# A pair of experts in the two column halves of TensorE, on whole float32 weights

## The chip, the cores and the metric

The kernel runs on one core of one Trainium2 chip. The metric is the device time of one execution in microseconds; a number of executions are timed, and one more is profiled. Products run on TensorE (PE, its weight loads PEld), the rest on VectorE (DVE), ScalarE (ACT) and GpSimd (POOL); SyncE (SP) issues the transfers.

## What is computed

Two transformer-like blocks on 512 tokens of 1024 features. The change lies in the last layer of the second block, an expert layer in which each of 16 experts takes the 64 tokens that have the greatest affinity to it. Cut to that layer:

```python
def expert_choice_ffn(h, w_router, w_gate, w_up, w_down):
    cap = EC_CAPACITY * L // N_EXPERTS                 # 2 * 512 // 16 = 64
    aff = jax.nn.softmax((h @ w_router).astype(jnp.float32), axis=-1)
    top_aff, top_idx = lax.top_k(jnp.swapaxes(aff, 1, 2), cap)
    xe = jax.vmap(lambda hb, ib: hb[ib])(h, top_idx)
    hid = jax.nn.silu(jnp.einsum('becd,edf->becf', xe, w_gate)) * jnp.einsum('becd,edf->becf', xe, w_up)
    ye = jnp.einsum('becf,efd->becd', hid, w_down) * top_aff[..., None].astype(h.dtype)
    combine = lambda ib, yb: jnp.zeros((L, D), yb.dtype).at[ib.reshape(-1)].add(yb.reshape(-1, D))
    return jax.vmap(combine)(top_idx, ye)
```

Each expert has three float32 matrices of 1024 x 1024 (gate, up, down), 201.3 MB for all 16.

## The kernel before

The residual stream lies with features on the partitions, in eight tiles `g.x` of 128 x 512. `moe` (line 1380) gets it tile by tile from `mixer_out` (line 1326), the output projection of the mixer ahead, and squares and scales each tile as it comes. Then the router's logits, the norm, and `route` (line 1343): softmax, the 64 greatest tokens of each expert by eight rounds of MAX8 and MATCH_REPLACE8, and by a scan the place of each token in each expert's list. The normed tokens are turned so that tokens lie on the partitions, in an upper part `e_ht` and a lower part `xh` (line 1473).

All large products of the kernel run in the one-pass format (float32r): an operand is split into an upper part, exact in that format, and a lower part, the rest (`split`, line 36: a copy on ScalarE, a subtraction on VectorE). The experts do it so:

- `stream` (line 1417) issues the weights in pieces of 256 rows (1 MiB, two row tiles `k`) into five places, two of the pool `wraw` and three of `e_raw`, and splits each row tile of 128 x 1024 into `whi` and `wlo`; `prepare` keeps three row tiles ahead of their use. The last two row tiles of each down matrix stay whole. A row tile is called a chunk below.
- `gather` (line 1482) makes one-hot tiles `e_oh` for the two experts of a pair and picks their tokens by products with `e_ht` and `xh`; the upper and the lower part of an expert's 64 tokens lie side by side as 128 stationary columns, in `e_x`. `turn` (line 1505) turns the one-hot tiles for later use and sorts the affinities.
- `product` (line 1521) makes [128, 1024] in two PSUM banks from eight row tiles: for a split tile 4 products of 128 stationary and 512 moving columns (upper and lower part of the weights, two halves `h` of the output), for a whole tile 2 products of 64 stationary columns, in float32. The two parts of an expert's rows come out on partitions 0 to 63 and 64 to 127.
- `activate` (line 1543) adds these two parts and turns them with products against a matrix `pair` (line 1549), makes silu(gate) * up with features on the partitions (silu by tanh) and splits the result into `e_hid`.
- The down product of an expert is scaled by the affinity on eviction and split into `xl` (lines 1589, 1590); `combine` (line 1561) adds a pair's rows to their tokens, per feature tile 4 products with the turned one-hot tiles `e_oht` and one accumulation on VectorE (line 1568).

The loop (line 1575) goes expert by expert: gate and up of expert e, then down of expert e - 1. `gather`, `turn`, `activate` and `combine` are generators in the queue `side`; `product` calls `side.pump()` after every second row tile, so that they come between the large products. A scheduler then sets the final order on each engine. `final` (line 1596) is the last norm and the stores.

## Time and profile before

| | us |
|---|---|
| median of 3 runs | 3245.01 |
| lowest, highest | 3242.98, 3249.72 |
| span of the profiled execution | 3242.7 |

| engine | busy us | share of the span |
|---|---|---|
| PE | 3108.6 | 96% |
| PEld | 2567.7 | 79% |
| DVE | 2098.0 | 65% |
| ACT | 1301.8 | 40% |
| POOL | 330.6 | 10% |

The span runs from the first to the last instruction of the profiled execution. That execution's own device time is not listed apart from its span; the three timed runs lie 0.3 to 7.0 us above the span, their median 2.3 us. "Busy" is the union of an engine's instructions; matmuls are pipelined and their ends are modelled, so a busy PE need not be at its peak, and the distance between starts tells its pace. DMA share is the mean busy share of the 16 DMA engines. The experts' stage is the last sixth of the span; the first five sixths are the first block and the mixer of the second.

### The profile page before, as it was taken

The numbers are of one execution on the slowest core, as the hardware profiler recorded it, in microseconds if no ns is written. First come the engines' busy times: TensorE is split into PE (matmuls) and PEld (weight loads), VectorE is DVE, ScalarE is ACT, GpSimd is POOL, SyncE is SP. The second block draws the span as 40 slices with busy tenths as digits, with TensorE's granted clock in tenths as the row PEclk, the third lists the DMA queues.
The fourth block names the chain that finished last, engine by engine and source line by source line (L and its number), as shares of the span: only waits on it lengthen the run. The fifth ranks groups of instructions, "written<-read, shape, count | busy, mean of one in ns | idle before, by whom it ended". The sixth has DMA issues, their size and how long they took to land. (4 is left out here: it accounts for less than half of the span.)

```text
span 3242.7 us, 40377 instructions
## 1 busy us (share of the span) xinstructions
PE 3108.6 (96%) x15866; PEld 2567.7 (79%) x15866; DVE 2098.0 (65%) x3258; ACT 1301.8 (40%) x1928; POOL 330.6 (10%) x256
## 2 busy tenths in 40 slices
PE   7999999999999999999998999999999789999997
PEld 6888888778888888887876888887889677777775
DVE  4444557654455896456766664447656569888887
ACT  3222335332223322233534322224322367777775
POOL 0101121010110020113102012011000210000000
PEclk9999999999999999999999999999999779999998
DMA  4432432123322674244212332223323249999995
GB/s 141 127 104 91 137 118 88 56 65 100 95 92 91 208 246 156 91 137 131 66 65 89 105 110 76 83 82 113 95 84 95 91 158 362 336 338 343 343 347 211
DMA packets 315347, 475.68 MB, mean 147 GB/s; under 512 B 32223, under 2 KB 244959, under 8 KB 312084
## 3 DMA queue, kind: packets, MB, share of 16 engines
q1 hardware_dynamic: 311768, 467.32, 42.8%
q10 hardware_dynamic: 2748, 3.68, 0.4%
q8 instruction: 124, 2.03, 0.3%
q0 software_dynamic: 640, 2.10, 0.2%
q14 instruction: 67, 0.55, 0.1%
HBM read 453.38 MB, written 19.67 MB: 146 GB/s over the span
## 5 line engine op out<-in xcount | busy, mean ns | idle before, releaser
L38 ACT CAST whi<-wraw 128x1024 fp32r<-128x1024 f32 (+4 forms) x532 | 535.0, 1016 | 1158.6 <-PE mm L68 892.3
L67 PE MATMUL mm<-xh,whi 128*128 128x512 f32 x1952 | 774.6, 399 | 11.2 <-ACT xh L135 8.3
L68 PE MATMUL mm<-xl,whi 128*128 128x512 f32 x1952 | 771.3, 395 | 0.8 <-DVE xl L136 0.6
L69 PE MATMUL mm<-xh,wlo 128*128 128x512 f32 x1952 | 768.7, 394 | 1.1 <-DVE wlo L39 1.1
L39 DVE TENSOR_TENSOR wlo<-wraw,whi 128x1024 fp32r<-128x1024 f32 (+4 forms) x532 | 680.9, 1289 | 110.1 <-ACT whi L38 93.9
L67 PEld LDWEIGHTS mm<-xh,whi 128*128 128x128 f32 x1952 | 371.1, 191 | 99.9 <-ACT xh L135 9.2
L68 PEld LDWEIGHTS mm<-xl,whi 128*128 128x128 f32 x1952 | 370.9, 190 | 80.4 <-issue 2.5
L69 PEld LDWEIGHTS mm<-xh,wlo 128*128 128x128 f32 x1952 | 371.0, 190 | 77.9 <-DVE wlo L39 1.9
L67 PE MATMUL mm<-hh,whi 128*128 128x512 f32 x704 | 278.8, 396 | 0.0
L69 PE MATMUL mm<-hh,wlo 128*128 128x512 f32 x704 | 277.9, 395 | 0.0
L68 PE MATMUL mm<-hl,whi 128*128 128x512 f32 x704 | 276.1, 392 | 0.0
L39 DVE TENSOR_TENSOR wlo<-e_raw,whi 128x1024 fp32r<-128x1024 f32 x210 | 249.2, 1221 | 32.5 <-ACT whi L38 31.8
L38 ACT CAST whi<-e_raw 128x1024 fp32r<-128x1024 f32 x210 | 212.3, 1050 | 31.1 <-PE mm L1531 29.0
L181 POOL TENSOR_TENSOR x<-x,dt 128x512 f32<-128x512 f32 x72 | 117.3, 1629 | 945.1 <-DVE dt L180 925.4
L161 DVE TENSOR_TENSOR gs<-mm,rb 128x512 f32<-128x512 f32 x88 | 60.8, 690 | 211.0 <-PE mm L69 206.6
L166 DVE TENSOR_TENSOR gs<-gs,mm 128x512 f32<-128x512 f32 x88 | 60.4, 686 | 194.0 <-PE mm L69 193.9
L180 DVE SCALAR_TENSOR_TENSOR dt<-mm,rb 128x512 f32<-128x512 f32 x104 | 71.8, 690 | 174.3 <-PE mm L69 174.2
L1531 PE MATMUL mm<-wlo,e_x 128*128 128x512 f32 x512 | 167.3, 408 | 2.1 <-DVE wlo L39 2.1
L1531 PE MATMUL mm<-whi,e_x 128*128 128x512 f32 x512 | 166.5, 407 | 1.6 <-DVE e_x L1501 1.3
L69 PEld LDWEIGHTS mm<-hh,wlo 128*128 128x128 f32 x704 | 132.2, 188 | 30.7
L68 PEld LDWEIGHTS mm<-hl,whi 128*128 128x128 f32 x704 | 132.3, 188 | 30.3 <-DVE hl L39 0.3
L67 PEld LDWEIGHTS mm<-hh,whi 128*128 128x128 f32 x704 | 132.4, 188 | 28.3
(623 smaller groups left out, 4630.4 us busy)
## 6 DMA issues: line engine op xcount, KB each, us to landing
wraw<-ffn_gate SPq DMA_DIRECT2D x44, 1024.0 KB, 5.4
wraw<-ffn_up SPq DMA_DIRECT2D x44, 1024.0 KB, 5.4
wraw<-w_in SPq DMA_DIRECT2D x38, 1024.0 KB, 5.3
e_raw<-e_gate SPq DMA_DIRECT2D x38, 1024.0 KB, 6.3
e_raw<-e_up SPq DMA_DIRECT2D x38, 1024.0 KB, 7.0
e_raw<-e_down SPq DMA_DIRECT2D x38, 1024.0 KB, 7.1
wraw<-e_gate SPq DMA_DIRECT2D x26, 1024.0 KB, 6.3
wraw<-e_up SPq DMA_DIRECT2D x26, 1024.0 KB, 6.9
```

The lines of the kernel that those rows point to most:

```text
L38: g.nc.scalar.copy(hi, src)
L39: g.nc.vector.tensor_sub(lo, src, f32(hi))
L67: g.nc.tensor.matmul(out, lh, rh, start=(i == 0), stop=False)
L68: g.nc.tensor.matmul(out, lh, rl, start=False, stop=False)
L69: g.nc.tensor.matmul(out, ll, rh, start=False, stop=(i == n - 1))
L161: nc.vector.tensor_mul(gs, pg, rb)
L166: nc.vector.tensor_mul(gs, gs, pu)
L180: nc.vector.scalar_tensor_tensor(t, pd, 0.25, rb, op0=OP.mult, op1=OP.mult)
L181: (nc.vector if c0 + nch == sum(groups) else nc.gpsimd).tensor_add(g.x[2 * c + m], g.x[2 * c + m], t)
L1531: nc.tensor.matmul(o, l, part[:, h * 512:(h + 1) * 512], start=(k + i == 0), stop=(k == NK - 1 and i == len(parts) - 1), skip_group_check= ...
```

## The change

Two experts, 2b and 2b + 1, form a pair b and work at the same time, expert 2b with 64 stationary columns in the left half of the array (output on partitions 0 to 63), expert 2b + 1 in the right half (partitions 64 to 127). Their weights are used whole, in float32, without a split. The inputs are laid out so that row tile k of both experts is one contiguous piece of 1 MiB, 8 KB on each partition (`host_inputs`). `load` has 12 places for such chunks: seven of `e_raw`, two of `wraw`, and three pairs of `whi` and `wlo` (two transfers each); the first loads are issued while `mixer_out` still runs. The tokens `ht` are float32 in one part, and the gather of a pair makes 128 columns, 64 of each expert. silu(gate) * up is made on token rows straight from the PSUM banks and turned by transposes (`turn_hidden`). A pair needs one turn of its one-hot tiles and, per feature tile, 2 products in `combine`. The gather and the turn of the first pair stand wholly ahead of the first product. `side.pump()` is called after every chunk.

```diff
+NR = 7
 def moe(g, I, P, x_out):
...
+    def load():
+        n = len(loaded)
+        w, b, k = chunks[n]
+        src = I["e_" + w][b, k]
+        place = n % (NR + 5) - (NR - 2)
+        if place < 2 or place >= 5:
+            raw = g.wraw.tile([128, 8 * WC], F32, name="wraw")[:, :2 * D] if 0 <= place < 2 else place_of()
+            raw = raw.rearrange("p (j c) -> p j c", j=2)
+            nc.sync.dma_start(raw, src)
+            loaded.append([raw[:, 0], raw[:, 1]])
+        else:
+            raw = [g.wsp.tile([128, 4 * WC], F32, name=nm)[:, :D] for nm in ("whi", "wlo")]
+            for j in range(2):
+                nc.sync.dma_start(raw[j], src[:, j])
+            loaded.append(raw)
...
+        if k in (1, 3, 5):
+            while len(loaded) < (NR - 2) * (k + 1) // 6:
+                load()
...
-        if k < 2:
-            nc.scalar.activation(xh[:, k, :], xw[k], AF.Identity, bias=shift[:, k:k + 1])
-            nc.vector.scalar_tensor_tensor(xl[:, k, :], xw[k], shift[:, k:k + 1], f32(xh[:, k, :]), op0=OP.add,
-                                           op1=OP.subtract)
-        else:
-            nc.scalar.activation(xw[k], xw[k], AF.Identity, bias=shift[:, k:k + 1])
-            nc.scalar.copy(xh[:, k, :], xw[k])
-            nc.gpsimd.tensor_sub(xl[:, k, :], xw[k], f32(xh[:, k, :]))
+        nc.scalar.activation(xw[k], xw[k], AF.Identity, bias=shift[:, k:k + 1])
...
     def gather(b):
...
+            for k in range(4):
+                f = 4 * q + k
+                for i in range(NT):
+                    nc.tensor.matmul(p[:, k * 128:(k + 1) * 128], ht[:, i, f * 128:(f + 1) * 128],
+                                     oh[:, i].rearrange("p j c -> p (j c)"), start=(i == 0), stop=(i == NT - 1))
...
+    def product(lhs):
         ps = [g.ps_m.tile([128, 512], F32, name="mm") for _ in range(2)]
         for k in range(NK):
-            prepare()
-            parts = ahead.pop(0)
-            for i, part in enumerate(parts):
-                for h in range(2):
-                    o, l = (ps[h], lhs(k)) if len(parts) > 1 else (ps[h][0:64], full(k))
-                    nc.tensor.matmul(o, l, part[:, h * 512:(h + 1) * 512], start=(k + i == 0),
-                                     stop=(k == NK - 1 and i == len(parts) - 1), skip_group_check=True)
-            if k % 2:
-                side.pump()
+            if used[0] == len(loaded):
+                load()
+            raw = loaded[used[0]]
+            used[0] += 1
+            for h in range(2):
+                for j in range(2):
+                    nc.tensor.matmul(ps[h][pj[j], :], lhs(k, j), raw[j][:, h * 512:(h + 1) * 512], start=(k == 0),
+                                     stop=(k == NK - 1), skip_group_check=True)
+            side.pump()
         return ps
...
+            pg = product(lambda k, j: xe[b][:, k, j, :])
+            hs = [P.tile([128, 512], F32, name="e_hs", bufs=4) for _ in range(2)]
+            for h in range(2):
+                th = P.tile([128, S], F32, name="e_full", bufs=2)
+                nc.scalar.activation(th, pg[h], AF.Tanh, scale=0.5)
+                nc.vector.scalar_tensor_tensor(hs[h], th, 1.0, pg[h], op0=OP.add, op1=OP.mult)
+            pu = product(lambda k, j: xe[b][:, k, j, :])
+            for h in range(2):
+                nc.vector.tensor_mul(hs[h], hs[h], pu[h])
+            side.q.insert(0, turn_hidden(b, hs))
+        if b:
+            d = b - 1
+            ps = product(lambda k, j: hid[d][:, k, j, :])
...
+            side.add(combine(d))
```

`pj` holds the partitions 0 to 63 and 64 to 127. How this stands on the engines, as the built programs have it:

TensorE inside the first gate product, before: L1531 are the products, `whi` and `wlo` the two parts of a chunk, `mm_19729` and `mm_19730` the two banks; L1497 is the gather.

```order
L1531 MATMUL mm_19729<-whi_19591,e_x_19709 128x512
L1531 MATMUL mm_19730<-whi_19591,e_x_19709 128x512
L1531 MATMUL mm_19729<-wlo_19592,e_x_19709 128x512
L1531 MATMUL mm_19730<-wlo_19592,e_x_19709 128x512
L1497 MATMUL sm_19743<-e_oh_19706,e_ht_19601 128x128
L1497 MATMUL sm_19743<-e_oh_19706,xh_19650 128x128 x4
L1497 MATMUL sm_19743<-e_oh_19706,e_ht_19601 128x128 x4
L1497 MATMUL sm_19743<-e_oh_19706,xh_19650 128x128 x4
```

The same place now; L1521 are the products (x2 is one of each half), L1485 the gather, L1497 and L1502 the turn. `whi` and `wlo` are here the weights of the two experts.

```order
L1485 MATMUL sm_19746<-e_oh_19712,xh_19595 128x128 x8
L1521 MATMUL mm_19706<-wraw_19516,e_x_19655 64x512 x2
L1521 MATMUL mm_19707<-wraw_19516,e_x_19655 64x512 x2
L1497 MATMUL sm_19772<-cst_96,e_oh_19712 128x128 x4
L1502 MATMUL sm_19779<-r_aff_19532,e_oh_19712 128x2 x4
L1521 MATMUL mm_19706<-wraw_19518,e_x_19655 64x512 x2
L1521 MATMUL mm_19707<-wraw_19518,e_x_19655 64x512 x2
L1521 MATMUL mm_19706<-whi_19520,e_x_19655 64x512
L1521 MATMUL mm_19706<-wlo_19521,e_x_19655 64x512
L1521 MATMUL mm_19707<-whi_19520,e_x_19655 64x512
L1521 MATMUL mm_19707<-wlo_19521,e_x_19655 64x512
```

A chunk has four products in both, then with 128 stationary columns in the one-pass format, now with 64 in float32, and those of the two halves alternate.

TensorE ahead of the first product, now: L1376 turns the selection, L1485 is the gather, L1497 and L1502 the turn of pair 0.

```order
L1376 MATMUL sm_19644<-cst_96,e_full_19592 128x16 x4
L1485 MATMUL sm_19656<-e_oh_19652,xh_19595 128x128 x16
L1485 MATMUL sm_19674<-e_oh_19652,xh_19595 128x128 x16
L1497 MATMUL sm_19692<-cst_96,e_oh_19652 128x128 x4
L1502 MATMUL sm_19699<-r_aff_19532,e_oh_19652 128x2 x4
L1521 MATMUL mm_19706<-e_raw_19243,e_x_19655 64x512 x2
```

Before, 19 of the gather's products (4, 4, 4, 4 and 3 rows of L1497) stood between the selection's turn and the first product.

SP at the start of the stage, now: L49 loads `w_out2` for `mixer_out`, L1405 and L1410 the experts' chunks; DVE, PE, Pool and Activation in the waits are those engines.

```order
L1405 DMA e_raw_19243<-e_gate 128x2048 [waits DMAHW0_49,PE_49,Pool_49]
L1405 DMA e_raw_19321<-e_gate 128x2048
L1405 DMA e_raw_19323<-e_gate 128x2048
L49 DMA wraw_19405<-w_out2 128x8x256 [waits DVE_49]
L1405 DMA wraw_19516<-e_gate 128x2048 [waits DVE_49]
L1405 DMA e_raw_19401<-e_gate 128x2048
L1405 DMA e_raw_19403<-e_gate 128x2048 [waits DMAHW2_49]
L1405 DMA wraw_19518<-e_gate 128x2048 [waits DMAHW7_49,DMAHW3_49,DVE_49]
L1410 DMA whi_19520<-e_gate 128x1024 [waits DMAHW4_49,PE_49]
L1410 DMA wlo_19521<-e_gate 128x1024 [waits DMAHW5_49,PE_49]
...
L1405 DMA e_raw_19824<-e_up 128x2048 [waits DMAHW4_49,PE_49]
L1405 DMA e_raw_19830<-e_up 128x2048 [waits DMAHW5_49,PE_49]
```

And before, where the places are freed by the split:

```order
L1431 DMA wraw_19883<-e_up 128x2x1024 [waits DMAHW2_49,DMAHW0_49,DVE_49]
L1431 DMA wraw_19905<-e_up 128x2x1024 [waits DMAHW3_49,DMAHW1_49,DVE_49]
L1431 DMA e_raw_19942<-e_up 128x2x1024 [waits DMAHW4_49,DVE_49]
L1431 DMA e_raw_19979<-e_gate 128x2x1024 [waits DMAHW5_49,DVE_49]
L1431 DMA e_raw_20021<-e_gate 128x2x1024 [waits DMAHW7_49,DVE_49]
```

In the running stage a load now waits for products (PE) where it waited for the split (DVE); besides, each transfer waits for the eighth one before it, whose semaphore (DMAHW0 to 7) it takes over.

## Rows read from the trace of the kernel before

**Rows 1.** Busy time by stage; us, busy of each engine, PEclk, DMA share, GB/s.

```profile
core 0: us, PE busy (x) PEld busy (x) DVE busy (x) ACT busy (x) POOL busy (x), PEclk, DMA share, GB/s
2620.00:3214.00 594.00, 586.32 (x2960) 456.39 (x2961) 514.24 (x537) 432.27 (x523) 0.00 (x0) 0.99 0.89 329
2640.00:3180.00 540.00, 535.81 (x2725) 418.81 (x2724) 475.74 (x498) 400.36 (x486) 0.00 (x0) 1.00 0.92 340
```

**Rows 2.** The chain in order of time, 2636 to 2662; start us, us, what.

```profile
2638.27 0.17 PE sm L1514 x2
2638.44 0.17 PE sm L1513
...
2647.28 1.74 PE sm L1497 x16
2649.02 1.91 PE mm L1531 x8
...
2654.59 3.52 PE sm L1549 x32
```

**Rows 3.** Timeline at two whole chunks; start us, us, engine, instruction, [idle before].

```profile
2687.62 0.19 PEld L1531 LDWEIGHTS mm<-e_raw,e_full 128*64 128x64 f32 x2 [0.37 <-issue]
2687.62 3.65 PE L1531 MATMUL mm<-e_raw,e_full 128*64 128x512 f32 x8
2688.11 0.14 PEld L1531 LDWEIGHTS mm<-e_raw,e_full 128*64 128x64 f32 x1 [0.29 <-issue]
...
2690.25 0.14 PEld L1531 LDWEIGHTS mm<-e_raw,e_full 128*64 128x64 f32 x1 [0.29 <-issue]
...
2691.20 0.30 PEld L1531 LDWEIGHTS mm<-whi,e_x 128*128 128x128 f32 x2 [0.81 <-ACT xl L1589]
```

**Rows 4.** Waits of the transfer queue, 2640 to 3180; total us, times, longest.

```profile
SPq L1431 <- DVE wlo L39: 390.5, 145, 5.0
```

**Rows 5.** Timeline at the modulation, four products in four column quarters.

```profile
1173.32 0.16 PEld L779 LDWEIGHTS sm<-mr,mfold 128*32 128x32 f32 x8 [0.36 <-issue]
1173.32 0.26 PE L779 MATMUL sm<-mr,mfold 128*32 128x16 f32 x8
```

**Rows 6.** Timeline of the stage's end.

```profile
3213.16 3.65 PE L1531 MATMUL mm<-wraw,e_full 128*64 128x512 f32 x8
3215.98 0.69 ACT L1589 ACTIVATE xl<-mm,e_aff 128x512 fp32r<-128x512 f32 x1 [5.85 <-PE mm L1531]
3216.70 1.61 DVE L1590 SCALAR_TENSOR_TENSOR xl<-mm,e_aff,xl 128x512 fp32r<-128x512 f32 x2 [4.75 <-ACT xl L1589]
```

**Rows 7.** Busy time in the stretches with the fastest transfers, columns as in rows 1.

```profile
3100.00:3120.00 20.00, 19.83 (x94) 15.98 (x92) 18.30 (x20) 13.67 (x16) 0.00 (x0) 1.00 1.02 404
2695.00:2700.00 5.00, 5.00 (x36) 4.55 (x36) 4.75 (x6) 3.24 (x4) 0.00 (x0) 1.00 1.02 417
```

**Rows 8.** Timeline ahead of the first expert product, VectorE and TensorE.

```profile
2592.11 0.98 DVE L1457 SCALAR_TENSOR_TENSOR xl<-e_x,mod,xh 128x512 fp32r<-128x512 f32 x1
2593.34 1.43 DVE L1457 SCALAR_TENSOR_TENSOR xl<-e_x,mod,xh 128x512 fp32r<-128x512 f32 x1 [0.24 <-ACT xh L1456]
2606.61 7.03 PE L1473 MATMUL sm<-cst2r,xl 128*128 128x128 f32 x32
2609.49 0.68 DVE L1371 TENSOR_TENSOR e_full<-e_full 16x512 f32<-16x512 f32 x1
2613.56 0.60 PE L1375 MATMUL sm<-cst,e_full 16*128 16x16 f32 x4
2614.46 1.29 DVE L1487 TENSOR_TENSOR e_oh<-r_place,cst 128x512 fp32r<-128x512 f32 x2
2615.91 1.09 PE L1497 MATMUL sm<-e_oh,e_ht 128*128 128x128 f32 x4 [1.74 <-DVE e_oh L1487]
2616.79 1.05 PE L1497 MATMUL sm<-e_oh,xh 128*128 128x128 f32 x4
2620.14 1.22 PE L1531 MATMUL mm<-whi,e_x 128*128 128x512 f32 x2
```

More of the change, by code (lines that the diff above doesn't have):

```diff
@@ L25 @@
 WC = 272
+NR = 7
 class G:
+    pass
 def f32(t):
@@ L1383, in moe, with place_of @@
     v = g.V2
-    NE = 16
+    NB = 8
     shift = g.mod[:, 24:32]
+    mats = [(w, b if w != "down" else b - 1) for b in range(NB + 1) for w in ("gate", "up", "down")]
+    chunks = [(w, b, k) for w, b in mats if 0 <= b < NB for k in range(NK)]
+    loaded = []
+    def place_of():
+        return P.tile([128, 2 * D], F32, name="e_raw", bufs=NR)
+    def load():
[13 more added lines that the diff above has]
+            loaded.append(raw)
     wr = g.wr
@@ L1477, in moe @@
+    next(routing)
+    ht = g.act.tile([128, NT, D], F32, name="xh")
+    for q in range(2):
+        for i in range(NT):
+            p = sm(g)
+            for k in range(4):
+                nc.tensor.transpose(p[:, k * 128:(k + 1) * 128], xw[4 * q + k][:, i * 128:(i + 1) * 128], g.ident)
+            nc.scalar.copy(ht[:, i, q * 512:(q + 1) * 512], p)
     next(routing)
-    affs = P.tile([128, NE], F32, name="e_aff")
+    affs = P.tile([128, NB], F32, name="e_aff")
+    ye = g.act.tile([128, 2, 2, D], F32R, name="xl")
@@ L1505, in turn @@
     def turn(b):
         oh = ohs[b]
+        p = sm(g)
+        for i in range(NT):
+            nc.tensor.transpose(p[:, i * 128:(i + 1) * 128], oh[:, i].rearrange("p j c -> p (j c)"), g.ident)
+        oht[b] = P.tile([128, S], F32R, name="e_oht", bufs=3)
+        nc.scalar.copy(oht[b], p)
         pa = sm(g)
+        for i in range(NT):
+            nc.tensor.matmul(pa[:, 0:2], oh[:, i].rearrange("p j c -> p (j c)"), aff[:, i, 2 * b:2 * b + 2],
+                             start=(i == 0), stop=(i == NT - 1))
@@ L1561, in combine, with turn_hidden @@
-    def combine(b, ye):
+            if used[0] == len(loaded):
+                load()
+            raw = loaded[used[0]]
[5 more added lines that the diff above has]
+            side.pump()
+        return ps
+    def turn_hidden(b, hs):
+        yield
+        hid[b] = P.tile([128, NK, 2, 64], F32, name="e_hid", bufs=2)
+        for q in range(2):
+            p = sm(g)
+            for k in range(4):
+                nc.tensor.transpose(p[:, k * 128:(k + 1) * 128], hs[q][:, k * 128:(k + 1) * 128], g.ident)
+            (nc.scalar.copy if q else nc.vector.tensor_copy)(
+                hid[b][:, 4 * q:4 * q + 4].rearrange("p k j c -> p (k j c)"), p)
+            yield
@@ L1569, in combine @@
             yield
-    ye = None
-    side.add(gather(0))
-    side.add(turn(0))
-    side.pump(2)
-    for e in range(NE + 1):
-        if e < NE:
-            if e < NE - 2:
-                side.add((turn if e % 2 else gather)(e // 2 + 1))
-            lhs = lambda k: xe[e // 2][:, e % 2, k, :]
-            cs = [to_sbuf(product(lhs)) for _ in range(2)]
-            side.q.insert(0, activate(e, cs))
-        if e:
-            d = e - 1
-            ps = product(lambda k: hid[d][0][:, k].rearrange("p s c -> p (s c)"), lambda k: hid[d][1][:, k, :])
-            if d % 2 == 0:
-                ye = g.act.tile([128, 2, 2, D], F32R, name="xl")
+    for gen in (gather(0), turn(0)):
+        for _ in gen:
+            pass
@@ new lines, in moe @@
+    for b in range(NB + 1):
+        if b < NB:
+            if b + 1 < NB:
+                side.add(gather(b + 1))
+                side.add(turn(b + 1))
+            pg = product(lambda k, j: xe[b][:, k, j, :])
[11 more added lines that the diff above has]
+            ps = product(lambda k, j: hid[d][:, k, j, :])
```

125 lines of the change are left out of this document (25 added, 100 removed).

## The prediction

> **What bounds the kernel now.** I read the busy time by stage first, then the chain of waits, then the timeline of the instructions that the change replaces, and last the waits of the transfer queue. The expert stage runs from 2620 to 3214 us, 594 of 3242.7 us, with TensorE busy for 586 of them at a granted clock of 0.99, and the transfers at a share of 0.89 and 329 GB/s [rows 1]. Two resources are near their limits there, so the next question is which one the other waits for. The chain of waits inside a pair consists of TensorE alone, piece after piece [rows 2], and its durations account for the stage. One pair of experts issues, by the code, 176 one-pass products of 512 columns for gate, up and down (44 chunks, 4 each), 16 instructions for the chunks that stay whole, 64 in the gather (L1497), 24 in `turn`, 64 in `activate` (L1549) and 32 in `combine`. The paces are 0.24 us for a one-pass product (1.91 for 8), 0.109 in the gather, 0.110 in `activate` and 0.11 in `turn` [rows 2]. A whole float32 product of 512 columns is recorded as two instructions, 0.428 us apart (five steps from 2688.11 to 2690.25) [rows 3]. That is 42.2 + 6.8 + 7.0 + 2.6 + 7.0 + 7.7 = 73.3 us a pair; 594 / 8 is 74.3. So TensorE sets the stage's end to within a per cent or two. The transfers wait: of the window of 540 us, the queue stood 390.5 us for VectorE's split to free a place [rows 4], and that split itself follows TensorE.
>
> **What the change does to TensorE.** All splitting goes, on ScalarE and VectorE; that is work beside the chain, so it gives nothing directly. What counts is a pair's TensorE time afterwards:
> - Products: 24 chunks with 4 products of 64 stationary columns, two instructions each: 192 x 0.428 = 82.2 us if the two halves take turns, 41.1 us if an instruction in one half runs beside one in the other. The trace of before has only one half in use at [rows 3], so this price is bounded from both sides. The nearest row is the modulation, which puts four products into four quarters of the columns: its eight weight loads lie in 0.16 us, although each is a load of over 0.1 us, and its eight products in 0.26 us [rows 5]. Eight instructions of the gather's pace would take 0.87 us. I take the full overlap, 41.1 us, and keep 82.2 as the other end.
> - Gather: 32 float32 products instead of 64 one-pass ones, two instructions each: 64 x 0.109 = 7.0 us, as before.
> - `turn`: 4 transposes and 4 small products of two instructions, 12 x 0.11 = 1.3 us. `turn_hidden`: 8 transposes, 0.9 us. `combine`: 16 x 0.24 = 3.8 us, half of before.
> - Going from full width to half width and back: the first weight load of [rows 3] stood 0.37 us where those inside the run stand 0.29, and behind the run the next load starts at 2691.20 where the last stream (2690.25 + 2 x 0.428) ends at 2691.11. I take 0.1 us each way; the order listing has ten such excursions a pair, 2.0 us.
> - The listing puts the first products of `combine` straight behind the down product whose result they need. They wait for its eviction: nothing at best, about 2.3 us at worst (0.69 us for a step on ScalarE and 1.61 for two on VectorE [rows 6]). I take 2.0 us.
>
> The sum is 41.1 + 7.0 + 1.3 + 0.9 + 3.8 + 2.0 + 2.0 = 58.1 us a pair against 73.3.
>
> **What it does to the transfers.** The bytes stay: 192 chunks of 1.0486 MB. What changes is who frees a place (TensorE's own products instead of the split) and how many there are: 12 chunks' worth instead of 5 and the three split pairs. So the queue has work ahead nearly always, where before it stood most of the time. With places free the rate was 404 GB/s over 20 us and 417 over 5 us; the mean of 540 us, with the waits, was 340 [rows 1, 7]. I take 404, because a queue that never waits is like that stretch: 2.60 us a chunk, 62.3 a pair. The ends of the range are 417 and 340. At 62.3 against 58.1 **the transfers become the bound**, with TensorE hidden behind them.
>
> The Trainium skill speaks against that rate: "DMA: Bandwidth & Descriptors", section "Where 436 GB/s comes from", says that for transfers between HBM and SBUF the HBM side binds, at about 358 GB/s for a core. The 404 GB/s of 20 us on this single core is above it, so here the measurement decides; by the page's figure the sum below would come to about 3182 us, an estimate.
>
> **The front of the stage.** Before, the first expert product starts at 2620.14 [rows 8]. VectorE loses two steps of the split norm (2592.11 to 2594.77): 2.7 us off the top-64 search. The selection's transpose at 2613.56 stood in TensorE's queue behind 32 turns of the lower part, though its input was there at 2610.17: 3.4 us. The one-hot tiles are half as wide: 0.6 us. So the first gather starts at 2615.91 - 6.7 = 2609.2. But now the whole gather and `turn` stand ahead of the first product, 64 and 12 instructions, where before 19 did. Each costs 0.21 us at the clock's lower level (4 in 0.88 at 2615.91) and 0.11 at the upper: 8.3 to 16 us, and 0.7 us for the copy. The first product starts between 2618 and 2626; I take 2623. During this front the transfers fill all 12 places, 31 us at 2.60, which starts while the output projection of the mixer still runs.
>
> **The sum.** 180 chunks remain at 2623. The first place comes free after one chunk's products (8 x 0.428 / 2 = 1.7 us), then 180 x 2.60 = 468 us, then the last chunk's products, 1.7 us: 3094.4. TensorE's own path, 2623 + 8 x 58.1 less the first gather and `turn` (8.3, already done) and the last `combine` (5.8, in the tail), ends at 3073.7, so 20 us of cover. The tail of before, from the end of the last product (3213.16 + 3.65) to 3242.7, is 25.9 us [rows 6]; it keeps its steps, evictions, eight accumulations on VectorE, the last norm and the stores, and I leave it. Span 3120.3 us; the median of the runs stands 2.3 us above the profiled span, so **3123 us**, 3.8% faster.
>
> **Rivals.**
> - *The transfers don't speed up* (0.13). With eight transfers under way packets could slow each other, and the rate stays at 340 GB/s [rows 1]: 180 x 3.08 = 555 us, 87 more, 3210 us. Against it, [rows 7] has a higher rate with TensorE just as busy; for it, the share there is already 1.02, so a queue that never waits cannot do more than in that stretch.
> - *The halves overlap, but weight loads don't run ahead* (0.12). In the order listing both instructions of one half stand before those of the other. If the load for the second half waits until the first half's second instruction has started, each step costs 0.428 + 0.14 (the load's length [rows 3]): 96 x 0.57 = 54.7 us a pair for the products, 71.7 in all, and TensorE stays the bound: 2623 + 8 x 71.7 - 14.1 + 25.9 + 2.3 = 3211 us. Inside one half the loads do run ahead: that at 2688.11 starts while the product before it streams. The Trainium skill, "TensorE: Matmul & The Clock Gate", section "Part 3: Packing small matmuls — row/col tiling", speaks for this rival: it says that weight loads overlap products under way only in another row group, and both halves here use all rows. The load at 2688.11 shares its rows with the product it overlaps, so the trace does not bear the rule out as it stands.
> - *The halves take turns* (0.12). Then the change does not do what it says, and TensorE pays 82.2 + 17.0 = 99.2 us a pair: 2623 + 8 x 99.2 - 14.1 + 28.2 = 3431 us, **slower by 6%**. It decides from the point where the products of a pair take over 59 us, that is where the overlap gains less than 1.4 times. For it: two float32 streams at once stand in no row, and [rows 5] has streams of 16 columns only, where loads and not streams set the pace.
>
> **How the numbers follow.** My forecast has 0.60, with a range of its own of 3098 to 3150 (417 GB/s and the earlier start at one end; TensorE's waits at pair ends not all covered, and the later start, at the other). The remaining 0.03 is for the granted clock falling to its lower level in the stage while the transfers starve TensorE; that would be slower too. The range reaches up over the first two rivals: 3098 to 3215 leaves out about 0.2. A measurement of this kernel can tell about 0.2% from no change. Faster: 0.60 + 0.13 + 0.12 = 0.85; slower: the third rival and most of the rest, 0.13; 0.02 for the middle.
>
> **What would show each step.** Right: starts of the 64-column products of the two halves in pairs, eight per chunk in about 1.7 us; the stage's DMA share near 1 and some 400 GB/s; idle TensorE time that ends on a transfer of `e_raw`, and the transfer queue waiting on products and not on a split; first product near 2623, last near 3094, tail 26 us. Wrong: eight instructions a chunk in 2.3 us (second rival) or 3.4 us (third), with TensorE full and the share of transfers below 0.8; a full share at 340 to 360 GB/s (first rival); a granted clock well under 1 between 2640 and 3080; a first product much after 2626, which moves the end by as much.

## The result and the profile after

The median fell from 3247.36 us (four runs) to 3114.11 us (four runs, 3109.66 to 3117.3): ratio 0.9592, 95% interval 0.9577 to 0.9607. The prediction was 3123 us; the measured time is 9 us below it and inside its range of 3098 to 3150. The profiled execution of the changed kernel took 3116.74 us, with a span of 3115.0 us.

The page of the changed kernel: span, busy time, the last two of its lines on the 40 slices, and the chain that ended last.

```profile
span 3115.0 us, 37508 instructions
...
PE 2973.3 (95%) x15162; PEld 2304.2 (74%) x15162; DVE 1666.3 (53%) x2864; ACT 891.5 (29%) x1442; POOL 319.8 (10%) x250
...
PEclk9999999999999999999999999999999988999998
DMA  4432343122323467224412233222323424999996
GB/s 145 130 98 95 107 141 110 47 70 90 95 95 95 137 215 256 95 94 143 130 53 75 83 108 112 79 86 78 111 70 94 122 109 177 413 417 418 417 419 274
...
PE 11%; DMA 6%; DVE 1%; POOL 0%; issue 0%; DVEq 0%; ACT 0%; SPq 0%; POOLq 0%
```

The last six slices are the experts' stage and the tail: the transfers' share stands at 9 (90% or more) in five of them and their rate at 413 to 419 GB/s. In the chain there are now transfers, 6% of the span. The page of the kernel before has none in its chain:

```profile
PE 17%; DVE 1%; ACT 0%; issue 0%; DVEq 0%; ACTq 0%
```

Line numbers move: the products are L1521 (before L1531), the gather L1485 (L1497), the turn L1497 and L1502, `turn_hidden` L1533, `combine` L1543 and L1544, the evictions L1571 and L1572 (L1589 and L1590), and the loads L1405 (a chunk in one transfer) and L1410 (in two).

Busy time by stage in the changed kernel, the columns of [rows 1].

```profile
core 0: us, PE busy (x) PEld busy (x) DVE busy (x) ACT busy (x) POOL busy (x), PEclk, DMA share, GB/s
2620.00:2640.00 20.00, 20.00 (x122) 11.45 (x123) 1.77 (x5) 1.23 (x3) 0.00 (x0) 1.00 0.70 263
2640.00:2700.00 60.00, 60.00 (x318) 26.05 (x317) 9.03 (x18) 4.73 (x8) 0.00 (x0) 1.00 0.99 395
2640.00:3060.00 420.00, 407.65 (x2028) 174.98 (x2025) 79.68 (x132) 29.58 (x49) 0.00 (x0) 1.00 1.01 415
2700.00:2800.00 100.00, 99.23 (x511) 46.05 (x508) 21.43 (x36) 8.44 (x14) 0.00 (x0) 1.00 1.02 417
```

From 2640 to 3060 the share of the transfers is 1.01 and their rate 415 GB/s; before it was 0.92 and 340 [rows 1]. TensorE has gaps now, 12.35 us of the 420. The first two rows matter below: at the front of the stage the rate is 263 GB/s, then 395.

A product's instructions in the changed kernel: TensorE's timeline where the tiles' names tell the two halves apart (`whi` in the left half, `wlo` in the right), and two pieces of the chain in order of time (start us, us, what).

```profile
2642.82 0.59 PE L1521 MATMUL mm<-whi,e_x 128*64 128x512 f32 x1
2642.82 0.59 PE L1521 MATMUL mm<-wlo,e_x 128*64 128x512 f32 x1
2643.24 0.59 PE L1521 MATMUL mm<-whi,e_x 128*64 128x512 f32 x1
2643.25 0.59 PE L1521 MATMUL mm<-wlo,e_x 128*64 128x512 f32 x1
2643.67 0.59 PE L1521 MATMUL mm<-whi,e_x 128*64 128x512 f32 x1
```

```profile
2635.89 1.98 PE sm L1485 x16
...
2641.12 20.75 PE mm L1521 x96
```

The records stand in pairs, one of each half, 0 to 10 ns apart, and the pairs follow one another every 0.43 us, the pace at which one half alone went before [rows 3]. 96 records, 12 chunks, take 20.75 us: 41.5 us for a pair's 24.

The waits of the changed kernel in the same stretch, for TensorE and for the transfer queue (total us, times, longest us).

```profile
PE mm L1521 <- DMA e_raw<-e_down: 3.5, 5, 1.4
PE mm L1521 <- DMA e_raw<-e_up: 2.7, 5, 0.6
```

```profile
SPq L1410 <- DMA e_raw<-e_up: 66.3, 33, 2.2
...
SPq L1405 <- PE mm L1521: 51.7, 44, 3.4
```

The queue no longer waits for VectorE's split [rows 4]. It waits for earlier transfers, and for the products that free a place only 64.6 us in 420 (51.7 at L1405 and 12.9 at L1410).

The stage's two ends in the timeline of the changed kernel, TensorE.

```profile
2610.53 9.01 PE L1485 MATMUL sm<-e_oh,xh 128*128 128x128 f32 x64 [1.20 <-DVE e_oh L1476]
2619.37 0.60 PE L1497 MATMUL sm<-cst,e_oh 128*128 128x128 f32 x4
2619.81 0.95 PE L1502 MATMUL sm<-r_aff,e_oh 128*128 128x2 f32 x8
2620.69 1.51 PE L1521 MATMUL mm<-e_raw,e_x 128*64 128x512 f32 x6
```

```profile
3083.61 1.94 PE L1521 MATMUL mm<-e_raw,e_hid 128*64 128x512 f32 x8 [0.53 <-DMA e_raw<-e_down]
3086.06 1.94 PE L1521 MATMUL mm<-e_raw,e_hid 128*64 128x512 f32 x8 [0.52 <-DMA e_raw<-e_down]
3087.93 2.13 PE L1543 MATMUL sm<-e_oht,xl 128*128 128x512 f32 x8
```

The first product starts at 2620.69 us. The last chunk's products wait 0.52 us for their transfer; the last record ends at 3088.0, and the rest is a tail of 27.0 us.

### The profile page after: what moved, and what is told of

It reads as the page before. It is cut to its first block, busy times and chain, and to the rows that moved or that the text cites. A ratio compares the mean times of both kernels' runs of the same rounds, so it can differ in the third digit from the quotient of the medians.

```text
span 3115.0 us, 37508 instructions
## 1 busy us (share of the span) xinstructions
PE 2973.3 (95%) x15162; PEld 2304.2 (74%) x15162; DVE 1666.3 (53%) x2864; ACT 891.5 (29%) x1442; POOL 319.8 (10%) x250
## 5 line engine op out<-in xcount | busy, mean ns | idle before, releaser
L39 ACT CAST whi<-wraw 128x1024 fp32r<-128x1024 f32 (+3 forms) x390 | 390.8, 1003 | 1116.9 <-PE mm L69 869.9
L40 DVE TENSOR_TENSOR wlo<-wraw,whi 128x1024 fp32r<-128x1024 f32 (+3 forms) x390 | 514.2, 1319 | 88.7 <-ACT whi L39 73.3
L227 PE MATMUL mm<-whi,xh 128*128 128x256 f32 (+1 forms) x448 | 131.5, 293 | 0.0
L229 PE MATMUL mm<-whi,xl 128*128 128x256 f32 (+1 forms) x448 | 128.8, 287 | 0.0
L228 PE MATMUL mm<-wlo,xh 128*128 128x256 f32 (+1 forms) x448 | 128.5, 287 | 0.0
L1521 PE MATMUL mm<-e_raw,e_x 128*64 128x512 f32 x536 | 123.1, 599 | 3.8 <-DMA e_raw<-e_up 2.7
## 6 DMA issues: line engine op xcount, KB each, us to landing
e_raw<-e_gate SPq DMA_DIRECT2D x26, 1024.0 KB, 12.6
```

The lines of the kernel that those rows point to most:

```text
L39: g.nc.scalar.copy(hi, src)
L40: g.nc.vector.tensor_sub(lo, src, f32(hi))
L227: nc.tensor.matmul(o, xh[:, kk, ts], wh, start=(kk == 0), stop=False)
L228: nc.tensor.matmul(o, xh[:, kk, ts], wl, start=False, stop=False)
L229: nc.tensor.matmul(o, xl[:, kk, ts], wh, start=False, stop=(kk == NK - 1))
L1521: nc.tensor.matmul(ps[h][pj[j], :], lhs(k, j), raw[j][:, h * 512:(h + 1) * 512], start=(k == 0), stop=(k == NK - 1), skip_group_check=True)
```

## Experiments

The start of the stage moves from one profiled execution to the next: among the changed kernel and the eleven runs made from it the first product starts between 2618.50 and 2633.53 us, and most of the edits touch nothing ahead of it. So besides the times, each run is compared by the distance from the start of its first product record to the start of its last, in its own trace. In the changed kernel that is 3087.41 - 2620.69 = 466.7 us. The runs were timed in several rounds, each beside the kernel before, whose median moved between 3246.61 and 3250.08 us; the ratio takes that out, and differences of a few us between medians of different rounds do not count.

| run | median us | ratio to before (95%) | first product | last product | between, us |
|---|---|---|---|---|---|
| the kernel before | 3247.36 | 1 | 2620.14 | 3216.21 | 596.1 |
| the changed kernel | 3114.11 | 0.9592 (0.9577 to 0.9607) | 2620.69 | 3087.41 | 466.7 |
| e1_half_outer | 3119.94 | 0.9607 (0.9584 to 0.9630) | 2620.83 | 3086.98 | 466.2 |
| e2_one_half | 3401.58 | 1.0474 (1.0449 to 1.0499) | 2630.37 | 3374.25 | 743.9 |
| e7_two_chunks_a_half | 3183.39 | 0.9795 (0.9778 to 0.9811) | 2633.53 | 3165.68 | 532.1 |
| e7_four_chunks_a_half | 3320.98 | 1.0233 (1.0216 to 1.0250) | 2620.07 | 3286.29 | 666.2 |
| e3_half_bytes | 3107.66 | 0.9573 (0.9554 to 0.9592) | 2620.60 | 3076.91 | 456.3 |
| e3b_seven_eighths | 3098.38 | 0.9549 (0.9534 to 0.9563) | 2622.52 | 3070.25 | 447.7 |
| e4_half_products | 3112.28 | 0.9584 (0.9563 to 0.9606) | 2625.40 | 3086.61 | 461.2 |
| b1_before_half_bytes | 3236.46 | 0.9970 (0.9957 to 0.9983) | 2629.03 | 3216.42 | 587.4 |
| e5_eight_places | 3131.70 | 0.9653 (0.9639 to 0.9667) | 2625.34 | 3102.47 | 477.1 |
| e6_two_transfers | 3128.98 | 0.9630 (0.9615 to 0.9644) | 2628.50 | 3104.71 | 476.2 |
| v3_first_product | 3119.88 | 0.9602 (0.9585 to 0.9620) | 2618.50 | 3086.25 | 467.7 |
| v4_late_gather | 3110.80 | 0.9579 (0.9563 to 0.9595) | 2629.77 | 3092.01 | 462.2 |

### Do the halves overlap because of their order?

**e1_half_outer.** The theory was that program order decides, the rival that each half takes its instructions by itself.

```diff
-            for h in range(2):
-                for j in range(2):
+            for j in range(2):
+                for h in range(2):
```

> The four products of a chunk are issued half by half (left half for both banks, then right half) instead of bank by bank. Theory: TensorE takes products in program order, and one starts early only while its neighbour ahead runs in the other half. Then of eight instructions a chunk only two pairs overlap, six steps of 0.429 us instead of four: 2.57 us a chunk, about 79 us a pair with the rest, TensorE becomes the bound, about 3267 us. Rival: each half has its own line and takes its products whenever it is free, so the order between the halves does not matter: no change from the changed kernel, about 3114 us.

Measured: 3119.94 us, ratio 0.9607, whose interval of 0.9584 to 0.9630 holds the changed kernel's 0.9592; 466.2 us between first and last product against 466.7. The theory fell. A run of 12 records in the trace lasts as long as six pairs: 2.85 us, five steps of 0.43 and 0.7 for the last pair.

```profile
2802.27 2.85 PE L1521 MATMUL mm<-e_raw,e_x 128*64 128x512 f32 x12
```

**e2_one_half.** All products behind the first chunk of each group of eight go to the left half; the sums of the right expert are left out.

```diff
-                    nc.tensor.matmul(ps[h][pj[j], :], ...
+                    nc.tensor.matmul(ps[h][pj[j if k == 0 else 0], :], ...
```

> From the second chunk of a product on, both experts' products go to the left half (the right expert's sums are left out, the left's are mixed); transfers, weight loads and all other work stay. Theory: the gain rests on the overlap of the halves, and without it a chunk costs eight steps of 0.429 us, 3.43 us (the first chunk of eight keeps four): about 95 us a pair, 3390 us, slower than the kernel before. Rival: the gain came from the places and the missing split, and the overlap matters little: under 3200 us.

Measured: 3401.58 us, 287 us above the changed kernel and slower than the kernel before. In its stage TensorE is busy without a gap and the transfers idle a quarter of the time (columns of [rows 1]):

```profile
2640.00:3060.00 420.00, 420.00 (x1310) 159.93 (x1308) 48.28 (x80) 18.87 (x31) 0.00 (x0) 1.00 0.75 266
```

So the same chunks, loads and products cost 4.7% more than before when the halves take turns: the whole gain rests on the overlap.

**e7_four_chunks_a_half and e7_two_chunks_a_half.** If e1's order costs nothing, how far apart may the halves stand? Four chunks (two, with 2 and 1 for 4 and 3) are collected, then used half by half:

```diff
-            raw = loaded[used[0]]
+            raws = raws if k % 4 else []
+            raws.append(loaded[used[0]])
             used[0] += 1
-            for h in range(2):
-                for j in range(2):
-                    nc.tensor.matmul(ps[h][pj[j], :], lhs(k, j), raw[j][:, h * 512:(h + 1) * 512], ...
+            for j in range(2 if k % 4 == 3 else 0):
+                for i, raw in enumerate(raws):
+                    for h in range(2):
+                        nc.tensor.matmul(ps[h][pj[j], :], lhs(k - 3 + i, j), raw[j][:, h * 512:(h + 1) * 512], ...
```

> The changed kernel with the order of a product's instructions changed: 16 instructions of the left column half (four chunks), then the 16 of the right half, and so on. If each half takes its instructions by itself, however far apart they stand: 3110 to 3128 (up to 4 chunks' places come free later, some 10 us). If TensorE can only look a few instructions ahead, the halves run apart for most of each group: up to 3 x 13.7 = 41 us more a pair, 8 pairs, less the cover of the transfers: 3300 to 3400.

Measured: 3320.98 us, 207 us more than the changed kernel and slower than the kernel before. The weight loads of that run show where one half ends and the other begins (the records are 0.43 us apart, the number behind the x is how many loads start together).

```profile
2803.56 0.14 PEld L1523 LDWEIGHTS mm<-e_raw,e_x 128*64 128x64 f32 x1 [0.29 <-issue]
2803.99 0.19 PEld L1523 LDWEIGHTS mm<-e_raw,e_x 128*64 128x64 f32 x3 [0.29 <-issue]
2804.42 0.19 PEld L1523 LDWEIGHTS mm<-e_raw,e_x 128*64 128x64 f32 x2 [0.24 <-issue]
2804.85 0.19 PEld L1523 LDWEIGHTS mm<-e_raw,e_x 128*64 128x64 f32 x2 [0.23 <-issue]
2805.33 0.14 PEld L1523 LDWEIGHTS mm<-wraw,e_x 128*64 128x64 f32 x1 [0.29 <-issue]
```

One load a step, so one half at a time; then seven loads in three steps, four of them for the half that begins; then one a step again. Only the last four records of one half's stretch run beside the first four of the other's. With 16 + 16 records that leaves most of the stretch single: counted in the trace, 1012 of the 1536 product records start without one of the other half beside them, against 4 in the changed kernel and in e1. The run with two chunks was forecast from that:

> The changed kernel with 8 instructions of the left column half (two chunks), then 8 of the right half, and so on. The run with 16 and 16 showed the halves side by side only for the last 4 instructions of a stretch. If that is what TensorE reaches ahead: of 8 and 8, 4 lie side by side at the change from left to right, 12 steps of 0.429 us in place of 8, and at the change from right to left as many where no other work is between: 4 x 0.429 x 4 x 3 = 20.6 us more a pair at most, 3098 + 165 = 3263 at most, 3180 where both borders overlap in half of the cases. If 8 instructions of a half are still within reach: 3110 to 3120.

Measured: 3183.39 us, 69 us more than the changed kernel, near the 3180 that was said for both borders overlapping in half of the cases. Here 368 of the 1536 records start alone, and the trace shows which. A piece of the timeline with no other work in it:

```profile
2799.59 10.32 PE L1523 MATMUL mm<-e_raw,e_hid 128*64 128x512 f32 x42
```

42 records one after the other would take 18 us. In this piece every record has a partner but the last four, because a stretch of eight pairs its first four with the end of the stretch before and its last four with the start of the next one. What stays single are the first and the last four records beside other work. So in these runs TensorE reaches four records ahead, and no further. The change's own order (two of one half, two of the other) and e1's (four and four) lie within that; eight and eight lose only where other work breaks the row, 16 and 16 in an unbroken row too.

### What sets the end now, and by how much?

**e3_half_bytes.** Half the transfers, to see TensorE alone.

```diff
-            if used[0] == len(loaded):
+            if used[0] // 2 == len(loaded):
                 load()
-            raw = loaded[used[0]]
+            raw = loaded[used[0] // 2]
```

> Each chunk that is loaded serves two steps of a product, so half of the experts' weights are left out and half of the bytes move; TensorE's work is unchanged. Theory: the transfers bind the stage from about 2755 us on and TensorE stands only for the 20 to 30 us in which it waits for them, so the time falls by that alone, to 3083 to 3097 us. Rival: TensorE or the evictions already set the pace: within 5 us of the changed kernel, 3109 to 3119. Second rival: the transfers cost far more, through contention: below 3070.

Measured: 3107.66 us, between the two forecasts, 1.3 us below the range of the first rival. But the run is not a clean one: with other loads the order of the work came out differently, and `combine` was cut into shorter pieces. The line of its products, in the changed kernel and in this run (duration ns min/median/max, first and last start):

```profile
L1543 PE MATMUL sm<-e_oht,xl x96: 391/397/505, 2712.6 to 3014.7; 128*128 128x512 f32 x96
```

```profile
L1543 PE MATMUL sm<-e_oht,xl x97: 397/496/500, 2714.2 to 3059.7; 128*128 128x512 f32 x97
```

In both traces the first of these products behind other work takes about 0.50 us and those behind it 0.40. In the changed kernel they come in pieces of 7, 6 and 3, in this run in pieces of 2, hence the median of 496 ns against 397. TensorE's work was thus longer than in the changed kernel, and this run can't tell by how much the transfers exceed it.

**e3b_seven_eighths** asks the same with TensorE's order nearly kept (the first `combine` comes in pieces of 2, the others in two or three pieces): only the load of a product's eighth chunk is left out.

```diff
-            if used[0] == len(loaded):
+            if k < NK - 1 and used[0] == len(loaded):
                 load()
-            raw = loaded[used[0]]
-            used[0] += 1
+            raw = loaded[used[0] - (k == NK - 1)]
+            used[0] += k < NK - 1
```

> The changed kernel with the eighth step of every product reading the seventh step's chunk again (the eighth chunk is not loaded, so one eighth of the experts' weights is left out), and TensorE's order of work all but as in the changed kernel. Transfers then need 21 x 2.515 = 52.8 us a pair and cannot bind, so the time is TensorE's own. If TensorE's sum of 58.1 us a pair was right, with the first product at 2620.7 and a tail of 26: 3093 to 3099 us. If a pair costs 1 us more than that (the gather's products were seen at 0.124 us in place of 0.109, and that alone is 1.0): 3100 to 3108. If transfers had not set the changed kernel's end at all: 3111 to 3117, no change.

Measured: 3098.38 us, inside the range for a TensorE sum of 58.1 us a pair, and 15.7 us below the changed kernel (14 by the ratios). Its stage has TensorE busy almost without a gap and the transfers below their full share:

```profile
2640.00:3060.00 420.00, 419.52 (x2094) 182.16 (x2090) 84.20 (x137) 31.40 (x52) 0.00 (x0) 1.00 0.96 380
```

Its chain over the same part (shares of the 451 us by engine and line) has no transfer in it, as the changed kernel's has; and this is all that TensorE waits for from 2622 to 3071 (total us, times, longest us):

```profile
by line: PE mm L1521 75.7%; PE sm L1485 12.9%; PE sm L1543 6.9%; PE sm L1533 1.8%; PE sm L1502 1.4%; PE sm L1497 0.9%; DVE e_hs L1564 0.3%; issue 0.1%
```

```profile
PE sm L1533 <- DVE e_hs L1564: 0.5, 2, 0.3
```

From first to last product 447.7 us: with all bytes it is 466.7, so the transfers lie 19 us above TensorE's own work.

**e4_half_products** is the other side: half of the products in six of a group's eight chunks are left out, the transfers stay.

```diff
-            for h in range(2):
+            for h in range(2 if k in (0, NK - 1) else 1):
```

> In the six middle chunks of each product the second bank's products are left out (its sums then cover two row tiles only); transfers are unchanged, TensorE's work falls by about 15.5 us a pair. Theory: the transfers bind, so the 124 us of TensorE's work that go give back only what the transfers waited for in the first 35 us of the stage, some 6 to 10 us: 3104 to 3110 us. Rival: TensorE sets the pace: about 120 us less, 2995 us.

Measured: 3112.28 us, 2.3 us above the forecast; ratio 0.9584: no difference to be told from 0.9592. In the trace, 461.2 us between the products, 5.5 less than with all of them. Its stage:

```profile
2640.00:3060.00 420.00, 357.05 (x1508) 142.76 (x1508) 79.84 (x132) 30.02 (x49) 0.00 (x0) 0.92 1.02 417
```

TensorE is idle for 63 of 420 us, and its granted clock is 0.92 there and not 1.00: for a part of the stretch it stood at the lower of its two levels. The rate of the transfers is 417 GB/s, 415 in the changed kernel. So the transfers set the end, and the 5.5 us are about what TensorE still adds to them; v4 below bears on where.

**b1_before_half_bytes** takes half of the bytes from the kernel before, by using each loaded piece twice.

```diff
-            for kp in range(4):
+            for kp in range(2):
...
-                for k in range(2):
-                    if w == "down" and kp == 3:
+                for kk in range(4):
+                    k = kk // 2
+                    if w == "down" and kp == 1 and kk >= 2:
```

> The kernel before, with each loaded quarter of a weight matrix used for two stretches of the product (half of the experts' weights are left out; the splits on VectorE, the products and their order are as before). If TensorE set the time before (586 of 594 us busy): within 10 us of the kernel before, 3238 to 3250. If the 340 GB/s of before were the bound: half the bytes would take off tens of us, under 3215.

Measured: 3236.46 us (ten runs), 0.3% below the kernel before, with an interval of 0.2 to 0.4%; 1.5 us below the range of the forecast. In the traces the stretch from first to last product is 587.4 us against 596.1. Half the traffic was worth 0.3% there, while 1/8 of it is worth 0.5% in the changed kernel. So the transfers did not bound the kernel before, though they cost it some 9 us. That it was TensorE and not the split on VectorE that did, this run does not tell, as it keeps both; that rests on the busy time, 586 of 594 us against 514 [rows 1].

### The transfers: places, packets, and the front of the stage

**e5_eight_places.**

```diff
-NR = 7
+NR = 3
```

> The changed kernel with 8 places for chunks in place of 12. If transfers set the end: 4 chunks fewer are there when the first product starts, 4 x 2.5 = 10 us, 3121 to 3128, and more if the 417 GB/s hang on how many transfers are under way. If TensorE sets the end: no change, 3110 to 3118.

Measured: 3131.70 us, 17.6 more than the changed kernel, above the forecast. The stage's own part is 477.1 - 466.7 = 10.4 us, the forecast 4 x 2.5; the rest is ahead of it (in this trace the first product is 4.7 us later), where the first loads stand elsewhere too, and is left open. Once under way the rate does not suffer from fewer places:

```profile
2620.00:2640.00 20.00, 20.00 (x138) 13.42 (x136) 2.46 (x6) 1.07 (x2) 0.00 (x0) 1.00 0.53 184
2640.00:3060.00 420.00, 408.33 (x2000) 182.57 (x1996) 77.56 (x129) 29.56 (x49) 0.00 (x0) 1.00 1.01 413
```

**e6_two_transfers.**

```diff
-            nc.sync.dma_start(raw, src)
+            for j in range(2):
+                nc.sync.dma_start(raw[:, j], src[:, j])
```

> The changed kernel with every chunk of an own place loaded by two transfers of 0.5 MiB in rows of 4 KB in place of one of 1 MiB in rows of 8 KB (as many transfers for these places as the split ones already take). Packets of 4 KB took 162 ns and packets of 8 KB 313 ns in the changed kernel, so the same bytes need 3.5% more of the queues' time: if transfers set the end, 2.515 becomes up to 2.60 us a chunk for the 7 to 10 places of 12 that change, some 150 chunks behind the first product: 7 to 13 us more, 3121 to 3127. If the rate of 417 GB/s is not that of the packets but of the memory: no change, 3109 to 3117.

Measured: 3128.98 us beside a kernel before of 3250.08, 2 us above the times forecast; the ratio is 0.0038 above the changed kernel's, 12 us. In the trace 476.2 us, 9.5 more, inside 7 to 13. The stage:

```profile
2640.00:3060.00 420.00, 413.18 (x2017) 188.40 (x2017) 76.42 (x129) 28.13 (x49) 0.00 (x0) 1.00 1.02 404
```

The share of the 16 engines is 1.02 at 404 GB/s, where with longer packets it was 1.01 at 415. It is the packets' own time that fills the engines (medians of 162 ns for 4 KB and 313 ns for 8 KB in the changed kernel): with shorter ones the same full share moves less.

**v3_first_product** was meant to start the stage earlier.

```diff
-    for gen in (gather(0), turn(0)):
-        for _ in gen:
-            pass
+    first = gather(0)
+    for _ in range(4):
+        next(first)
+    side.add(first)
+    side.add(turn(0))
```

> The changed kernel with the first pair's gather cut: only its first half is done ahead of the first product, its second half and the turn of the one-hot go between products. The first product then starts some 5 us earlier, and with it the refill of the 12 places, which had stood full before it. If transfers set the end: 3 to 6 us less, 3107 to 3111. If the transfers of these 5 us were not lost before (hidden anyway): no change, 3112 to 3116.

Measured: no gain, 3119.88 us, above both forecasts; ratio 0.9602 (interval 0.9585 to 0.9620). Of the gather's 64 records 48 still stand ahead of the first product:

```profile
2611.34 7.22 PE L1485 MATMUL sm<-e_oh,xh 128*128 128x128 f32 x48 [1.20 <-DVE e_oh L1476]
```

So the first product, at 2618.50, came 7.2 us behind the start of the gather against 10.2 in the changed kernel, 3.0 us earlier and not 5, and the stage took 467.7 us, 1.0 more. What was taken from ahead of the first product now stands between the first chunks, where it delays the places that come free.

**v4_late_gather** goes after those refills. The issues of the transfer queue in the changed kernel (L1405 is the load) show their pace:

```profile
2622.67 9.74 SPq L1405 DMA_DIRECT2D e_raw<-e_up  x4
2635.93 0.33 SPq L1405 DMA_DIRECT2D e_raw<-e_gate  x1
2639.78 3.57 SPq L1405 DMA_DIRECT2D wraw<-e_gate  x2
```

Seven refills lie between 2622.67 and 2643.03, most of them 3.85 us apart: a chunk's products (1.87) and 16 gather products for the second pair (1.98) between two freed places. A transfer takes 1.0486 MB / 417 GB/s = 2.51 us.

```diff
-            if b + 1 < NB:
-                side.add(gather(b + 1))
-                side.add(turn(b + 1))
-
-            pg = product(lambda k, j: xe[b][:, k, j, :])
+            for late in range(2):
+                if late == (b == 0) and b + 1 < NB:
+                    side.add(gather(b + 1))
+                    side.add(turn(b + 1))
+                if late == 0:
+                    pg = product(lambda k, j: xe[b][:, k, j, :])
```

> The changed kernel with the second pair's gather put behind the first gate product (it stood between that product's chunks); all other work and its order stay. In the changed kernel the first products took 3.85 us a chunk with that gather between them, and the refills of the 12 full places were issued at that pace from 2624.39 to 2639.78 (263 GB/s from 2620 to 2640, 395 to 2700, where 417 came later: together some 10 us of transfers lost). Without it a chunk takes 1.87 us, below the 2.51 us of a transfer. If transfers set the end from the first product on: 5 to 8 us less, ratio to the kernel before 0.9567 to 0.9577, last product 5 to 8 us earlier after the first. If these transfers are made up for later (TensorE sets the end often enough): no change, 0.959 or above.

Measured: the refills come 1.72 us apart (the first product of this trace is 9.1 us later than the changed kernel's, for reasons ahead of the edit):

```profile
2631.74 5.48 SPq L1405 DMA_DIRECT2D e_raw<-e_up  x4
2638.61 0.33 SPq L1405 DMA_DIRECT2D e_raw<-e_gate  x1
```

Between the products 462.2 us, 4.5 less, a little under the 5 to 8 forecast. The time is 3110.80 us, ratio 0.9579 against 0.9592, outside the forecast by 0.0002 and with intervals that overlap: the saving is seen in the trace and not proven by the times. v4 has the lowest ratio of the versions that do all the work, but it isn't shown to beat the change.

## Why the prediction was right, point by point

- **The halves overlap, 41.1 us a pair**: right; 41.5 measured. The choice of 41.1 and not 82.2 rested on the modulation's streams of 16 columns [rows 5]; that it holds for 512 columns no row of before could show, so it was an extrapolation that came true. e2 puts the other end on the chip, though a product's first chunk of eight still overlaps in it: 3402 us where the rival of halves that take turns said 3431.
- **Weight loads run ahead**: right, and that rival fell: 0.43 us a step and not 0.57. The order of the halves, on which the rival rested, is free within about four records (e1 against the two e7 runs). The Trainium skill, "TensorE: Matmul & The Clock Gate", section "Part 3: Packing small matmuls — row/col tiling", says that a weight load overlaps a product under way only in another row group; here both halves use all rows, and a pair follows the other every 0.43 us with weight loads of 0.14 us in every step, so they lie beside products under way, and the trace does not agree.
- **TensorE's sum, 58.1 us a pair, and its own path of 2623 to 3073.7, 450.7 us**: right as a sum. e3b shows 448.3 from its first product to the end of its last. Inside it the terms were off both ways. Low: 16 products of the gather take 1.98 us, 0.124 each and not 0.109, so 7.9 us a pair and not 7.0; by the shares of e3b's chain the products take 42.7 us a pair and `combine` 4.4 (seven fall in the stretch), where 41.1 and 3.8 were said. High: the sum has 2.0 us a pair for changes of width, most of which is already in these measured times, and 2.0 us for waits of `combine` for an eviction, and there TensorE waits 0.5 us in all eight pairs. That these cancel was luck.
- **The transfers become the bound with 20 us of cover**: right. 19 us (466.7 against e3b's 447.7), seen from both sides: with an eighth of the bytes gone the time falls by 15.7 us, with 124 us of TensorE's work gone (three eighths of 41.2 us a pair) it does not change measurably.
- **Their price, 2.60 us a chunk at 404 GB/s**: too high. From 2700 to 2800 the rate is 417 GB/s, 2.515 us; 180 chunks take 452.7 us and not 468. The 5 us of [rows 7] that showed 417 came nearer than the 20 us at 404. What the sum left out is the length of the rows: the pieces of the kernel before have 4 KB on each partition, nine of the 12 places now 8 KB, and e6, which puts 4 KB back there, has 409 GB/s in those 100 us, which is most of the difference. The rival at 340 GB/s fell with it, and e6 shows what the 417 hang on: the share stays full when the rate drops. The Trainium skill, "DMA: Bandwidth & Descriptors", section "Where 436 GB/s comes from", says that the memory side binds at about 358 GB/s, which it derives as half of the 716 GB/s of a stack that two cores share, and gives beside it a measured 425 GB/s for one transfer of 16 MB. The 415 GB/s over 420 us of this single core are above the first figure and near the second, so the 358 was not the one to hold against this kernel.
- **"180 x 2.60 from the first freed place on"**: this is the step that failed. The queue did have to wait behind the first freed place, for places that came free every 3.85 us, and the end is short of the full rate too. In the changed kernel, from its first refill on and at the last transfers (columns of [rows 1]):

```profile
2622.67:2640.00 17.33, 17.33 (x107) 10.00 (x104) 0.69 (x1) 0.59 (x1) 0.00 (x0) 1.00 0.81 303
3080.00:3086.00 6.00, 5.02 (x24) 1.45 (x19) 0.00 (x0) 0.00 (x0) 0.00 (x0) 1.00 0.54 226
```

  303 GB/s over 17.3 us and 395 over the 60 behind them are short of 417 by 17.3 x 114/417 + 60 x 22/417 = 4.7 + 3.2 = 7.9 us, and 226 over the last 6 us by 2.7. With the 2.0 us from the first product to the first refill, 180 chunks in 452.7, and 1.4 from 3086.0 to the start of the last product, the stage's sum is 2.0 + 452.7 + 7.9 + 2.7 + 1.4 = 466.7, as measured. The forecast of 471.4 (to the end of the last product, where the trace has 467.3) came close by luck: the rate was set too low by 15.3 us, and the front and the end were overlooked by 10.6. v4 gives 4.5 of the 7.9 back.
- **First product at 2623, tail of 25.9**: 2620.69, for a gather at 2610.53 (2609.2 said) and 10.2 us from there, in the lower part of the 8.3 to 16 allowed: the granted clock was 0.66 from 2610 to 2615 and 1.00 from there on. The tail was 27.0.
- **The clock at its lower level while transfers starve TensorE (0.03)**: did not happen, 1.00 from 2640 to 3060 with 12 us of gaps. In e4, with 63 us of gaps, it was 0.92, and the time did not rise, because the transfers set it.

In sum, 2620.7 + 467.3 + 27.0 = 3115.0 us of span against 3120.3.

## What to carry to other kernels

When two resources are within some per cent of each other, work out both paths to the end: the gain of such a change is cut off by the second one, here 19 us above the first. In a stage that the transfers bound, the queue has to be busy from the start: with all places full ahead of it, what stands between the first products that free a place is paid in transfers, even where TensorE has cover. Two independent streams in two column halves need no exact interleaving, but their instructions must stand within a few of each other (four records here), and longer stretches lose where other work breaks their row.

## What was not expected of the hardware

- The halves of the array run side by side when the program gives two or four records of one and then as many of the other; with eight and eight they still do in an unbroken row, but the time rises by 69 us, with 16 and 16 by 207.
- With 12 places to fill a single transfer of 1 MiB takes 12.6 to 15.0 us from issue to landing (medians of the changed kernel's page, below, `e_gate` 12.6; those of the same size in an earlier stage take 5.4), and the rate is nevertheless at its highest of the whole run. So here the landing time of one transfer does not tell the bandwidth. The issues of the changed kernel (count, KB each, us to landing):

```profile
e_raw<-e_down SPq DMA_DIRECT2D x45, 1024.0 KB, 13.8
wraw<-ffn_gate SPq DMA_DIRECT2D x44, 1024.0 KB, 5.4
...
e_raw<-e_up SPq DMA_DIRECT2D x41, 1024.0 KB, 15.0
...
e_raw<-e_gate SPq DMA_DIRECT2D x26, 1024.0 KB, 12.6
```
